# A two-layer SWA, mLSTM and FoX trunk: layer 0's attention stage regrouped with a gate block between its parts and q, k turned by DMA, layer 1's last joins and scores placed earlier

## The chip, the cores and the metric

The kernel runs on one core of a Trainium2 chip. The core has five engines, each with its own instruction stream: TensorE (PE, matmuls; PEld is its weight load), VectorE (DVE), ScalarE (ACT), GpSimd (POOL) and SyncE (SP, which here only issues DMAs). The metric is the device time of one execution in microseconds, as the median of several runs.

## The reference

A trunk of two residual layers over 256 tokens of width 2048, in fp32. Each layer is a mixer and a SwiGLU feed-forward block of hidden width 5632, each behind an RMSNorm. Layer 0's mixer splits one projection into a sliding-window attention (16 query heads of 64, 4 key heads, window 128) and an mLSTM (4 heads, q and k of 128, v of 256); layer 1's mixer is a causal attention with a forget-gate bias (16 heads of 128).

```python
def swa_mlstm_mixer(xn, w_in, w_out, sinks, b_i, b_f, head_gain):
    proj = xn @ w_in
    q_s, k_s, v_s, q_m, k_m, v_m, o_m, i_m, f_m = split_cols(proj, EVEN_SIZES)
    attn = sliding_window_attention(q_s, k_s, v_s, sinks)        # heads reshaped
    i_pre = softcap(i_m + b_i)
    f_pre = softcap(f_m + b_f)
    h = mlstm_chunkwise(q_m, k_m, v_m, i_pre, f_pre)             # chunks of 128
    h = rms_norm(h, head_gain)
    mem = jax.nn.sigmoid(o_m) * h
    return jnp.concatenate([attn, mem], axis=-1) @ w_out
...
def forgetting_attention_mixer(xn, w_in, b_f, w_out):
    q, k, v, f = split_cols(xn @ w_in, FOX_SIZES)
    c = cumsum(log_sigmoid(f + b_f))
    s = q @ k.T * scale + c[:, None] - c[None, :]                # causal mask
    return softmax(s) @ v @ w_out
```

## The kernel before

Every fp32 product is made of three fp32r products. A chunk of weights (256 rows by 512 columns, 512 KB) is loaded by SP into one of four `raw` buffers (L117, `load_raw`); ACT casts it to `hi` (L169), DVE subtracts to `lo` (L170), both in `split_chunk`; PE then does hi by hi, lo by hi and hi by lo (L197 to L199 in `gemm`). A chunk in `gemm` is 12 matmuls of 512 columns: two row blocks, two halves of the tokens, three products. Activations are kept split too, as `xh`, `xl` for the normed input and `mh`, `ml` for the mixer's output; `split_plain` (L295 on ACT, L296 on DVE) makes those. Where two projections of the same input are due (q with k, the two halves of v), `pair_group` does them with seven products instead of eight per two by two blocks; it needs four banks for `plain`, four for `prods`, and at its end `c` is put together from `prods` (L551 to L555) and `fold` adds `plain` (L684, L685). PSUM has two pools of four banks, `pa` (tag acc) and `pm` (tag pm). Names such as `h<-prod` in the profile stand for `c` where a tile lies in the room of another.

Layer 0's order before: K and V of the sliding-window attention, the first eight query heads (`acc1`), then groups 0 and 1 one after the other (`swa(g, qn)`: scores with L319 and L326, softmax with exps L349 on ACT and the products with 1/den L362 on DVE, transposes of the probabilities L371 and L375 copied by ACT L372 and DVE L376, products with v L379 and L380), then the second projection of queries, and groups 2 and 3 with two gate blocks of 256 columns (`tacc`, `oacc`) between their steps. The mLSTM's gates follow: sigmoid (L806), tanh, exp and ln on ACT, the prefix sums through small matmuls `pu`, `pn`, `pb` (L827 to L870), two scans on DVE, the decay matrix `dt_` (L873, L881). Then the q,k group, whose 16 blocks and four of `qsc` are transposed on PE (`ptm`, L307) and copied by DVE (L308), with the 512-column gate block `oacc` in pieces between them; then the scores `pq` (L927), the value group, and the heads with the first chunks of the output projection `begun0`.

Layer 1 has four groups of four heads. q and k of a group are turned by DMA: `turn_heads` copies the two 16-bit halves of each number to planes (ACT, L1094), SP issues a DMA transpose for each plane (L248), and `join` puts them together (two copies for each of q and k, ACT, L1103). The starts and joins of a group are handed out as `steps` during the next group's work; for the last group they are issued in a `while` loop after the last `values` and `begin` parts. `begin(m, k0, k1)` does k0 to k1 of the layer's output projection for column block m; `attend` is a generator whose steps are scores and softmax, transposes, products with v.

The order on each engine comes from the tile scheduler, which orders instructions by data, buffers and a timeline of its own; `tc.issue_after(ins)` puts what is issued inside behind a given instruction. Engines run their streams in order, so an instruction that waits holds all behind it on its engine. `raw` has four buffers, `hi` and `lo` six; the `raw` of pairs (`rb`) come from a room of two.

Of the kernel before, what the change touches and what calls it, by code (L numbers as in the profile page):

```python
# [7 lines left out]
F32 = mybir.dt.float32  # L8
# [9 lines left out]
P = 128  # L18
D = 2048
S = 256  # L20
# [44 lines left out]
def trunk(  # L65
# [94 lines left out]
    last_exp = [None]  # L160

# [4 lines left out]
    def split_chunk(raw, n):  # L166
        hi = wp.tile([P, CK, NB], F32R, tag="hi", name="hi")
        lo = wp.tile([P, CK, NB], F32R, tag="lo", name="lo")
        latest[0] = nc.scalar.copy(hi[:, :, 0:n], raw[:, :, 0:n])  # L169
# [124 lines left out]
    def split_plain(dst_h, dst_l, src):  # L294
        nc.scalar.copy(dst_h, src)  # L295
        nc.vector.tensor_tensor(out=dst_l, in0=src, in1=dst_h.bitcast(F32), op=ALU.subtract)  # L296
# [13 lines left out]
    def attention(sp, q_of, k_of, v_of, dv, scale, bias0, bias1, k_tile, sinks=None, negc=None, s=None, ps=((pm, "pm"), (pm, "pm"))):  # L310
# [48 lines left out]
        for b in range(NT):  # L359
            for j in range(4):  # L360
                e = s[j % 2][:, j // 2, parts[b]]
                nc.vector.tensor_scalar(e, e, rec[:, b, j : j + 1], None, op0=ALU.mult)  # L362
# [132 lines left out]
    def pair_group(room, par, lhs, sums, mats, order, todo=(), row=lambda k: k):  # L495
# [5 lines left out]
        for pos, (kind, pair) in enumerate(order):  # L501
# [21 lines left out]
            hg, lg = split_chunk(ra, NB)  # L523
            run_due(todo, pos)
            t4 = room.t4()
            nc.vector.tensor_tensor(out=t4[:, 0, :], in0=rb[:, 0, :], in1=ra[:, 0, :], op=ALU.subtract)
            nc.vector.tensor_tensor(out=t4[:, 1, :], in0=rb[:, 1, :], in1=rb[:, 0, :], op=ALU.subtract)
            hu = wp.tile([P, CK, NB], F32R, tag="hi", name="hi")
            lu = wp.tile([P, CK, NB], F32R, tag="lo", name="lo")
            split_plain(hu[:, 1, :], lu[:, 1, :], rb[:, 1, :])  # L530
# [176 lines left out]
    with tc.tile_pool(name="ev", bufs=1) as ev:  # L707
# [21 lines left out]

        with tc.tile_pool(name="sw", bufs=1) as sw:  # L730
# [62 lines left out]
            gemm(oacc, x_of, wi, c_o, 256, 0, 4, KT)  # L793
            next(two, None)
            gemm(oacc, x_of, wi, c_o, 256, 4, 8, KT)
            next(three_)
            gemm(oacc, x_of, wi, c_o, 256, 8, 12, KT)
            next(three_, None)
            gemm(oacc, x_of, wi, c_o, 256, 12, KT, KT)

        og = ev.tile([P, NT, ML_H * VD], F32, name="og")

        def gate_out(acc, c0, n):
            for t in range(NT):
                o = og[:, t, c0 : c0 + n]
                nc.scalar.activation(o, acc[t][:, 0:n], AF.Sigmoid, scale=r[:, t : t + 1])  # L806
                nc.gpsimd.tensor_tensor(out=o, in0=o, in1=gain[:, c0 : c0 + n], op=ALU.mult)

        acc = tacc
        gates = ev.tile([P, NT, 8], F32, name="gates")  # L810
        for t in range(NT):
            nc.vector.scalar_tensor_tensor(
                out=gates[:, t, :], in0=acc[t][:, 256:264], scalar=r[:, t : t + 1], in1=bias_g, op0=ALU.mult, op1=ALU.add
            )
        gate_out(acc, 768, 256)
        gate_out(oacc, NB, 256)
        nc.scalar.activation(gates, gates, AF.Tanh, scale=1.0 / CAP)
        nc.vector.tensor_scalar(gates, gates, CAP, None, op0=ALU.mult)
        ig = gates[:, :, 0:4]
        nlf = ev.tile([P, NT, 4], F32, name="nlf")  # L820
        nc.scalar.activation(nlf, gates[:, :, 4:8], AF.Exp, scale=-1.0)
        nc.scalar.activation(nlf, nlf, AF.Ln, bias=1.0)

        pu = pm.tile([P, NB], F32, tag="pm", name="pu")
        for c in range(NT):
# [468 lines left out]
```

## Time and profile before

Three runs: 2096.64, 2095.11 and 2090.21 us, median 2095.11.

| | us |
|---|---|
| profiled execution | 2096.03 |
| its span | 2094.3 |
| PE busy | 2080.2 |
| DVE busy | 1810.2 |
| ACT busy | 1365.8 |
| weights and other reads from HBM | 408.67 MB, 196 GB/s over the span |

The page gives busy times of engines, the chain that ended last and groups of instructions. Matmuls are pipelined: a matmul of 512 columns has a record of 0.39 us, while the next one starts 0.23 us later, so lengths of PE's work are taken from start to start. The granted clock of TensorE is 1.00 or 0.50; at 0.50 matmuls take twice as long. fp32 matmuls that are not fp32r stand twice in the trace (two passes), once in the program. Rows of the chain of waits name what an engine waited for, in order of time; "DMA raw" there is the time from a load's issue to its landing.

### The profile page before, as it was taken

The numbers are of one execution on the slowest core, as the hardware profiler recorded it, in microseconds if no ns is written. First come the engines' busy times: TensorE is split into PE (matmuls) and PEld (weight loads), VectorE is DVE, ScalarE is ACT, GpSimd is POOL, SyncE is SP. The second block draws the span as 40 slices with busy tenths as digits, with TensorE's granted clock in tenths as the row PEclk, the third lists the DMA queues.
The fourth block names the chain that finished last, engine by engine and source line by source line (L and its number), as shares of the span: only waits on it lengthen the run. The fifth ranks groups of instructions, "written<-read, shape, count | busy, mean of one in ns | idle before, by whom it ended". The sixth has DMA issues, their size and how long they took to land.

```text
span 2094.3 us, 26757 instructions
## 1 busy us (share of the span) xinstructions
PE 2080.2 (99%) x9502; PEld 1727.9 (83%) x9502; DVE 1810.2 (86%) x2400; ACT 1365.8 (65%) x1721; POOL 41.1 (2%) x70
## 2 busy tenths in 40 slices
PE   9999999999999999999999999999999999999998
PEld 7878888888888888888888888788888888888886
DVE  6688758999999998998898777579999999998995
ACT  6565568766567655766867676586766567556763
POOL 2100000000000000000000000000000000000000
PEclk9999999999999999999999999999999999999999
DMA  9446667766676757676787665577766677658763
GB/s 331 120 135 190 215 183 229 249 194 214 205 227 214 215 195 223 212 221 172 205 259 209 201 212 164 170 232 228 241 204 215 197 220 212 228 179 227 220 200 132
DMA packets 304438, 434.56 MB, mean 207 GB/s; under 512 B 102049, under 2 KB 110257, under 8 KB 304305
## 3 DMA queue, kind: packets, MB, share of 16 engines
q1 hardware_dynamic: 302544, 427.05, 65.7%
q0 software_dynamic: 1616, 5.78, 0.8%
q8 instruction: 74, 1.21, 0.2%
q14 instruction: 60, 0.48, 0.1%
q10 hardware_dynamic: 144, 0.03, 0.0%
HBM read 408.67 MB, written 2.11 MB: 196 GB/s over the span
## 4 chain that ended last, share of the span: by engine, by line
PE 94%; DMA 2%; DVE 2%; ACT 1%; issue 1%; SPq 0%; POOLq 0%; POOL 0%; ACTq 0%
PE acc L421 20%; PE acc L420 20%; PE acc L422 20%; PE prod L420 5%; PE prod L421 5%; PE prod L422 5%; PE acc L197 4%; PE acc L199 4%; PE acc L198 4%; PE vacc L199 1%; PE vacc L197 1%; PE vacc L198 1%; DMA raw<-in_w_out_odd_dram 1%; DVE lo L170 1%; PE p L326 0%
## 5 line engine op out<-in xcount | busy, mean ns | idle before, releaser
L169 ACT CAST hi<-raw 128x1024 fp32r<-128x1024 f32 (+1 forms) x664 | 674.4, 1031 | 430.0 <-PE acc L422 247.9
L170 DVE TENSOR_TENSOR lo<-raw,hi 128x1024 fp32r<-128x1024 f32 (+1 forms) x664 | 783.8, 1195 | 149.2 <-ACT hi L169 146.5
L421 PE MATMUL acc<-lo,xh 128*128 128x512 f32 x1204 | 468.7, 389 | 0.5 <-DVE lo L170 0.5
L422 PE MATMUL acc<-hi,xl 128*128 128x512 f32 x1204 | 464.7, 389 | 0.0
L420 PE MATMUL acc<-hi,xh 128*128 128x512 f32 x1204 | 462.1, 389 | 0.0
L421 PEld LDWEIGHTS acc<-lo,xh 128*128 128x128 f32 x1204 | 226.1, 188 | 47.9 <-DVE lo L170 0.8
L422 PEld LDWEIGHTS acc<-hi,xl 128*128 128x128 f32 x1204 | 226.1, 188 | 47.2 <-issue 0.3
L420 PEld LDWEIGHTS acc<-hi,xh 128*128 128x128 f32 x1204 | 226.1, 188 | 46.9
L421 PE MATMUL acc<-lo,mh 128*128 128x512 f32 x444 | 172.7, 389 | 0.0
L422 PE MATMUL acc<-hi,ml 128*128 128x512 f32 x444 | 171.4, 389 | 0.0
L420 PE MATMUL acc<-hi,mh 128*128 128x512 f32 x444 | 169.3, 389 | 0.0
L295 ACT CAST ht<-raw 128x1024 fp32r<-128x1024 f32 x94 | 98.8, 1051 | 58.9 <-DVE raw L532 22.4
L197 PE MATMUL acc<-hi,mh 128*128 128x512 f32 x320 | 126.6, 398 | 3.1 <-ACT mh L295 3.1
L198 PE MATMUL acc<-lo,mh 128*128 128x512 f32 x320 | 125.7, 393 | 0.0
L199 PE MATMUL acc<-hi,ml 128*128 128x512 f32 x320 | 125.0, 393 | 0.0
L295 ACT CAST ht<-t 128x1024 fp32r<-128x1024 f32 x94 | 98.8, 1052 | 39.6 <-PE prod L422 29.3
L296 DVE TENSOR_TENSOR lt<-raw,ht 128x1024 fp32r<-128x1024 f32 x94 | 114.4, 1217 | 5.5 <-ACT ht L295 5.3
L296 DVE TENSOR_TENSOR lt<-t,ht 128x1024 fp32r<-128x1024 f32 x94 | 114.3, 1216 | 1.2 <-ACT ht L295 0.9
L295 ACT CAST hi<-raw 128x512 fp32r<-128x512 f32 x112 | 69.3, 619 | 63.9 <-PE acc L422 48.6
L421 PEld LDWEIGHTS acc<-lo,mh 128*128 128x128 f32 x444 | 83.4, 188 | 17.3
L420 PEld LDWEIGHTS acc<-hi,mh 128*128 128x128 f32 x444 | 83.3, 188 | 17.3
L422 PEld LDWEIGHTS acc<-hi,ml 128*128 128x128 f32 x444 | 83.3, 188 | 17.3
(375 smaller groups left out, 3571.0 us busy)
## 6 DMA issues: line engine op xcount, KB each, us to landing
raw<-in_w_gate_dram SPq DMA_DIRECT2D x176, 512.0 KB, 4.7
raw<-in_w_up_dram SPq DMA_DIRECT2D x176, 512.0 KB, 4.8
raw<-in_w_down_dram SPq DMA_DIRECT2D x176, 512.0 KB, 5.1
raw<-in_w_in_odd_dram SPq DMA_DIRECT2D x88, 512.0 KB, 4.8
raw<-in_w_in_even_dram SPq DMA_DIRECT2D x64, 512.0 KB, 4.6
raw<-in_w_out_even_dram SPq DMA_DIRECT2D x32, 512.0 KB, 4.3
raw<-in_w_out_odd_dram SPq DMA_DIRECT2D x32, 512.0 KB, 5.2
raw<-in_w_in_odd_dram SPq DMA_DIRECT2D x8, 272.0 KB, 3.5
```

What stands on the lines that cost most here:

```text
L169: latest[0] = nc.scalar.copy(hi[:, :, 0:n], raw[:, :, 0:n])
L170: nc.vector.tensor_tensor(out=lo[:, :, 0:n], in0=raw[:, :, 0:n], in1=hi[:, :, 0:n].bitcast(F32), op=ALU.subtract)
L197: nc.tensor.matmul(o, ah[:, ts], hi, start=(k == 0), stop=False)
L198: nc.tensor.matmul(o, ah[:, ts], lo, start=False, stop=False)
L199: last_mm[0] = nc.tensor.matmul(o, al[:, ts], hi, start=False, stop=(k == k_all - 1))
L295: nc.scalar.copy(dst_h, src)
L296: nc.vector.tensor_tensor(out=dst_l, in0=src, in1=dst_h.bitcast(F32), op=ALU.subtract)
L420: nc.tensor.matmul(o, ah, hi, start=start, stop=False)
L421: nc.tensor.matmul(o, ah, lo, start=False, stop=False)
L422: nc.tensor.matmul(o, al, hi, start=False, stop=stop)
```

## The change

It has four parts. (1) Layer 0's sliding-window groups run in pairs: 0 and 1 begin together and the second query projection stands between their steps; 2 and 3 likewise with the gate blocks. (2) The gates' functions move ahead, and the 512-column gate block (`oacc`, OFF_OM) moves from behind the q,k group to between groups 2 and 3, the prefix matmuls and the exps. (3) q and k of the mLSTM are turned by DMA as in layer 1: ACT copies planes to `qmt` and `kmt`, four DMA transposes land in the rooms of `ce` and `ve`, four ACT copies join; starts and joins are handed to the value group (`TURN_QK` = its first four pair steps), and the scores `pq` and the transposes of `qsc` come after that group. The q,k group takes the other bank pools (par 1 for 0). (4) In layer 1, the last group's joins are issued one at a time at parts 5 and 6 of the last loop, the next split of a chunk is held behind each, the last group's scores come before `begin(0, 8, 10)`, and `begin(1, ...)` is cut at 2 and 6 instead of 6 and 10. `late` and `last_mul` are new and not used.

```diff
     def split_chunk(raw, n):
...
-        latest[0] = nc.scalar.copy(hi[:, :, 0:n], raw[:, :, 0:n])
+        with ExitStack() as order:
+            if behind[0]:
+                order.enter_context(tc.issue_after(behind[0].ins))
+                behind[0] = None
+            latest[0] = nc.scalar.copy(hi[:, :, 0:n], raw[:, :, 0:n])
...
-            for g in range(2):
-                for _ in swa(g, qn):
-                    pass
-            qn = natural(sw, project(wi, OFF_QS + NB, NB), NB, "qn")
+            zero, one = swa(0, qn), swa(1, qn)
+            next(zero)
+            next(one)
+            qacc = project(wi, OFF_QS + NB, NB)
+            for gen in (zero, one):
+                next(gen)
+                next(gen, None)
+            qn = natural(sw, qacc, NB, "qn")
...
-            gemm(tacc, x_of, wi, c_t, 264, 0, 2, KT)
             next(two)
-            gemm(tacc, x_of, wi, c_t, 264, 2, 6, KT)
             next(three_)
-            gemm(tacc, x_of, wi, c_t, 264, 6, KT, KT)
+            gemm(tacc, x_of, wi, c_t, 264, 0, KT, KT)
+            gemm(oacc, x_of, wi, c_o, 256, 0, 4, KT)
             next(two)
...
+            gate_out(oacc, NB, 256)
+            oacc = new_acc()
+            gemm(oacc, x_of, wi, OFF_OM, NB, 0, 4, KT)
             next(three_)
-            gemm(oacc, x_of, wi, c_o, 256, 8, 12, KT)
+            gemm(oacc, x_of, wi, OFF_OM, NB, 4, 6, KT)
             next(three_, None)
...
+            gemm(oacc, x_of, wi, OFF_OM, NB, 6, 10, KT)
...
         nc.scalar.activation(ex, ex, AF.Exp)
-
+        gemm(oacc, x_of, wi, OFF_OM, NB, 10, 14, KT)
...
+            gemm(oacc, x_of, wi, OFF_OM, NB, 14, KT, KT)
+            gate_out(oacc, 0, NB)
...
-            plain, c = pair_group(room, 0, x_of, sums_m, [(wi, OFF_QM), (wi, OFF_KM)], QK_ORDER)
+            plain, c = pair_group(room, 1, x_of, sums_m, [(wi, OFF_QM), (wi, OFF_KM)], QK_ORDER)
             fold(plain, c, (rq, r))
-            oacc = [bank(1, "oacc") for _ in range(NT)]
-            gemm(oacc, x_of, wi, OFF_OM, NB, 0, 6, KT)
...
+                for b in range(2):
+                    nc.scalar.copy(flat[:, b, :].rearrange("p (t n) -> p t n", t=NT), cu[:, 2 * m : 2 * m + 2, :, b])
+
+                def start(flat=flat, turned=turned):
+                    with tc.issue_after(load[0].ins):
+                        turn_planes([turned[:, b, :, :] for b in range(2)], flat)
+
+                def join(whole=whole, turned=turned):
+                    cb = whole.rearrange("p (n b) -> p n b", b=2)
+                    for b in range(2):
+                        nc.scalar.copy(
+                            cb[:, :, b].rearrange("p (g t q) -> p g t q", g=4, t=NT),
+                            turned[:, b, :, :].rearrange("p (t g) q -> p g t q", t=NT),
+                        )
...
-            for dst, src in ((qmt, qm), (kmt, km)):
-                for g in range(0, ML_H, 2):
-                    transpose_many(
-                        dst[:, g : g + 2, :].rearrange("p g (t q) -> p (g t) q", q=P),
-                        [src[:, t, (g + i) * QK : (g + i + 1) * QK] for i in range(2) for t in range(NT)],
-                        (pa, "acc"),
-                    )
...
-            plain, c = pair_group(room, 0, x_of, sums_m, [(wi, OFF_VM), (wi, OFF_VM + NB)], QK_ORDER)
+            plain, c = pair_group(
+                room, 0, x_of, sums_m, [(wi, OFF_VM), (wi, OFF_VM + NB)], QK_ORDER, list(zip(TURN_QK, starts + joins))
+            )
...
+                if i == 3 and n in (5, 6):
+                    with tc.issue_after(last_exp[0].ins):
+                        run_next(steps)
+                    behind[0] = last_join[0]
                 part()
...
-        while steps:
-            with tc.issue_after(last_exp[0].ins):
-                run_next(steps)
+        split2 = last_split[0]
         begun[1] = new_acc()
...
-        begin(0, 8, 10)
         with tc.issue_after(last_mm[0].ins):
             next(gen)
+        begin(0, 8, 10)
+        behind[0] = split2
         begin(0, 10, 12)
-        begin(1, 0, 6)
+        begin(1, 0, 2)
         next(gen)
-        begin(1, 6, 10)
+        begin(1, 2, 6)
         next(gen, None)
-        begin(1, 10, 12)
+        begin(1, 6, 12)
```

How the scheduler's order moves is shown at three places. The first is ACT in layer 1, from the exps of the third group on (a row is an operation, `hi<-raw` a cast of a weight chunk, `heads` a join, `t<-pp` the copy of the transposed probabilities, `mh<-po` the split of the attention's output). Before, L-numbers of the kernel before:

```order
L349 ACTIVATE s,den<-s,neg 128x256 x4
L169 CAST hi<-raw 128x1024 x4
L1103 COPY heads<-t_11220 128x1024 x2
L1103 COPY heads<-turned 128x1024 x2
L372 COPY t_11453<-pp 128x512 x2
L169 CAST hi<-raw 128x1024 x5
L295 CAST mh<-po 128x512 x2
L1036 ACTIVATE vn<-vacc,r 128x256 x2
```

And now (L1130 is the join, L176 the cast):

```order
L356 ACTIVATE s,den<-s,neg 128x256 x4
L176 CAST hi<-raw 128x1024
L1130 COPY heads<-t_11208 128x1024 x2
L176 CAST hi<-raw 128x1024
L1130 COPY heads<-turned 128x1024 x2
L176 CAST hi<-raw 128x1024 x2
L379 COPY t_11441<-pp 128x512 x2
L176 CAST hi<-raw 128x1024
L302 CAST mh<-po 128x512 x2
```

The four joins stood together behind four casts; now one cast stands ahead of the first two, one between the pairs, and five casts in place of nine stand ahead of `mh`.

The second place is PE in layer 0, at the prefix matmuls (`pu`, `pn`, `pb` are the gates' small products, `acc<-hi,xh` and its like a chunk of the 512-column gate block, `po` the products with v). Before:

```order
L380 MATMUL po<-t_1232,vs 64x128
L845 MATMUL pn<-ident,mt 128x4
L846 MATMUL pn<-ident,edge 128x4
L844 MATMUL pn<-nlf,upper 128x4
L845 MATMUL pn<-ident,mt 128x4
L846 MATMUL pn<-ident,edge 128x4
L870 MATMUL pb<-mt,sel 128x256 x4
L420 MATMUL acc<-hi,s_1388 128x512
L421 MATMUL acc<-lo,s_1388 128x512
```

And now:

```order
L204 MATMUL acc<-hi,xh 128x512
L205 MATMUL acc<-lo,xh 128x512
L859 MATMUL pn<-ident,mt 128x4
L860 MATMUL pn<-ident,edge 128x4
L858 MATMUL pn<-nlf,upper 128x4
L859 MATMUL pn<-ident,mt 128x4
L860 MATMUL pn<-ident,edge 128x4
L887 MATMUL pb<-mt,sel 128x256 x4
L206 MATMUL acc<-hi,xl 128x512
L204 MATMUL acc<-hi,xh 128x512
```

`pu`, which before directly preceded these with eight rows of `po`, now lies 28 matmuls of the gate block ahead of the first `pn` with `mt`; the q,k group that followed `pb` at once now follows ten more matmuls.

The third place is the value group, on SP (loads of weight chunks and the DMA transposes) and on ACT (`qmt<-h` the plane copies of q, `qmt<-ce` the joins). SP now, where before stood 38 loads from `in_w_in_even` in a row and no transposes:

```order
L117 DMA raw<-in_w_in_even_dram 128x2x512 x32
L255 DMA_TRANSPOSE ce<-qmt 128x8x128 x2
L255 DMA_TRANSPOSE ve<-kmt 128x8x128 x2
L117 DMA raw<-in_w_in_even_dram 128x2x512 x6
L117 DMA raw<-in_w_out_even_dram 128x2x512 x23
```

ACT now:

```order
L927 COPY qmt<-h 128x1024 x2
L927 COPY kmt<-h 128x1024 x2
L176 CAST hi<-raw 128x1024
L302 CAST mh<-raw 128x1024
L176 CAST hi<-raw 128x1024
L936 COPY qmt<-ce 128x1024 x2
L302 CAST hi<-raw 128x512
L936 COPY kmt<-ve 128x1024 x2
L302 CAST mh<-h 128x1024
L176 CAST hi<-raw 128x1024 x2
```

The last six loads of the group stand behind the four transposes on SP, and the casts of the group's later chunks stand behind the joins on ACT. PE loses its 16 `ptm<-ident,h` transposes.

More of the change, by code (lines that the diff above doesn't have):

```diff
@@ L798, in trunk @@
             next(three_, None)
[L799 to L810, printed above, removed]
@@ L821, in trunk @@
[L821 to L825, printed above, removed]
-            uo = pu[0:4, c * P : (c + 1) * P]
-            nc.tensor.matmul(uo, ig[:, c, :], ident, start=True, stop=False)
-            nc.tensor.matmul(uo, nlf[:, c, :], upper, start=False, stop=True)
-        nc.tensor.matmul(pu[0:4, 2 * P : 2 * P + 1], nlf[:, 0, :], ones[:, 0:1], start=True, stop=True)
@@ L839, in trunk @@
[L839 to L841 removed]
+            pu = pm.tile([P, NB], F32, tag="pm", name="pu")
+            for c in range(NT):
+                uo = pu[0:4, c * P : (c + 1) * P]
+                nc.tensor.matmul(uo, ig[:, c, :], ident, start=True, stop=False)
+                nc.tensor.matmul(uo, nlf[:, c, :], upper, start=False, stop=True)
+            nc.tensor.matmul(pu[0:4, 2 * P : 2 * P + 1], nlf[:, 0, :], ones[:, 0:1], start=True, stop=True)
```

138 lines of the change are left out of this document (78 added, 60 removed).

## The prediction

> **What bounds the kernel now.** I read the page's head and busy times first, then the chain of waits, then a windows view cut at the changes of the granted clock.
>
> ```profile
> span 2094.3 us, 26757 instructions
> PE 2080.2 (99%) x9502; PEld 1727.9 (83%) x9502; DVE 1810.2 (86%) x2400; ACT 1365.8 (65%) x1721; POOL 41.1 (2%) x70
> PE 94%; DMA 2%; DVE 2%; ACT 1%; issue 1%; SPq 0%; POOLq 0%; POOL 0%; ACTq 0%
> ```
>
> PE is busy for 99% of the span and holds 94% of the chain, so an edit can gain in two ways only: fewer matmuls, or less of PE's time lost to waits and half clock. How much is lost, and where, the windows show (columns: stretch, length, then busy us and instructions of PE, PEld, DVE, ACT, POOL, then the granted clock, DMA share, GB/s).
>
> ```profile
> 80.00:143.37 63.37, 62.71 (x428) 52.55 (x428) 52.50 (x108) 43.47 (x98) 5.59 (x8) 1.00 0.48 146
> 143.37:146.78 3.41, 3.41 (x26) 2.90 (x23) 2.49 (x11) 1.10 (x2) 0.11 (x1) 1.00 0.00 0
> 146.78:150.19 3.41, 3.41 (x9) 2.26 (x8) 2.91 (x10) 2.54 (x9) 0.00 (x0) 0.50 0.00 0
> 150.19:153.60 3.41, 3.41 (x10) 2.64 (x9) 2.71 (x6) 2.94 (x5) 0.00 (x0) 0.50 0.00 0
> 153.60:300.00 146.40, 146.40 (x671) 121.23 (x670) 112.42 (x157) 80.44 (x111) 9.24 (x10) 1.00 0.63 194
> 300.00:1140.00 840.00, 840.00 (x3755) 697.65 (x3754) 768.39 (x978) 570.59 (x661) 4.21 (x6) 1.00 0.70 215
> 1310.73:1314.14 3.41, 1.22 (x6) 0.79 (x5) 1.67 (x3) 2.56 (x5) 0.00 (x0) 1.00 0.82 293
> 1314.14:1317.55 3.41, 3.41 (x9) 2.72 (x9) 2.16 (x3) 1.17 (x2) 0.00 (x0) 0.50 0.90 324
> ```
>
> Most of the kernel runs as the row from 300 us does: 3755 matmuls in 840 us, 0.224 us each, with nothing to win. The two layers' attention stages are the exception. In layer 0 PE idles 63.37 - 62.71 = 0.66 us before 143.4, and from 146.78 it runs 6.82 us at clock 0.50, which costs half of that, 3.41. So at most 4.1 us can come back there. Ahead of the half clock stands a stretch of 26 tiny matmuls (143.37), in layer 1 one with PE busy for 1.22 of 3.41 us. Either can take the clock down.
>
> In layer 1 the chain of waits (start, length, what) and PE's timeline tell why:
>
> ```profile
> 1299.40 1.14 ACT heads L1103
> 1300.62 2.96 ACT heads L1103 x3
> 1304.25 1.05 ACT t L372 x2
> 1305.30 0.96 ACT hi L169
> 1306.28 1.24 DVE lo L170
> 1307.53 3.94 DMA raw<-in_w_out_odd_dram
> 1311.58 1.04 ACT hi L169
> 1312.62 0.49 ACT mh L295
> 1318.46 0.23 PE acc L199
> 1335.22 7.44 DMA raw<-in_w_out_odd_dram
> 1342.77 1.04 ACT hi L169
> ```
> ```profile
> 1310.58 0.39 PE L199 MATMUL acc<-hi,ml 128*128 128x512 f32 x1
> 1313.16 0.50 PE L197 MATMUL acc<-hi,mh 128*128 128x512 f32 x1 [2.19 <-ACT mh L295]
> 1344.35 0.50 PE L197 MATMUL acc<-hi,mh 128*128 128x512 f32 x1 [0.88 <-ACT mh L295]
> ```
>
> ACT first does four joins in a row (1.14 + 2.96 us), so the casts of the weight chunks start 5 us late, the raw slots come free late, the load that goes into one of them lands late (1307.53 + 3.94), and the cast that waits for it stands ahead of `mh` on ACT, for which PE waits. A matmul of 512 columns takes 0.23 us from start to start, so PE could have gone on at 1310.81 and went on at 1313.16: 2.35 us lost. The window at half clock behind it loses 1.71, and the second place of the same kind 0.88. Layer 1's stock is therefore 4.9 us.
>
> **The change part by part.** *Transposes removed.* 16 transposes of q and k leave PE.
>
> ```profile
> 186.13 1.69 PE L307 MATMUL ptm<-ident,h 128*128 128x128 f32 x14
> ```
>
> 14 of them, the last 0.27 long by the tile's own row, take (1.69 - 0.27)/13 = 0.11 us each: -1.8 us. This is sure, since PE is the bound. DVE loses four copies, off the path.
>
> *Layer 1's joins.* Each join now stands between casts: cast, two joins, cast, two joins, casts. The joins' 4.1 us are the same, and the third chunk's `lo` comes 0.6 us after PE asks for it by my walk through the new order with these rows' lengths; then casts and loads run ahead. Between the last group's scores and its transposes there are now 87 matmuls (19.7 us) instead of 55. Behind these transposes only 3 matmuls (0.7 us) stand before the products with v, which need ACT's two copies (1.05 us, row 1304.25) and a DVE copy of 0.7; the copies start while the last seven transposes (0.8 us) still run, so that wait is at most 0.3. I take -4.9 + 0.6 = -4.3. Bounds: -4.9 if nothing waits, and -1 if the late load only moves (the long landing of 7.44 us against 3.94 is 3.5 us, more than the lead that a cast gains).
>
> *Layer 0's attention and the filler.* The 512-column gate block (96 matmuls) moves from behind the q,k group to between the small matmuls of groups 2 and 3 and the gates. In the new order the `pn` rows have chunks of it on both sides, so a stretch like 143.37 disappears and with it the half clock: up to -4.1. What comes in exchange is DVE. Between the `s`-by-`rec` products of group 3 and the second `dt_` addition, DVE now has the gate prefix, two `t4` subtractions that wait for weight loads, and five splits.
>
> ```profile
> 138.33 1.93 DVE L362 TENSOR_SCALAR s<-s,rec 128x128 f32<-128x128 f32 x8
> L170 DVE TENSOR_TENSOR lo<-raw,hi 128x1024 fp32r<-128x1024 f32 x27 | 32.5, 1217 | 4.6 <-ACT hi L169 4.4
> L526 DVE TENSOR_TENSOR h<-raw 128x512 f32<-128x512 f32 x5 | 3.4, 683 | 0.1
> raw<-in_w_in_even_dram SPq DMA_DIRECT2D x64, 512.0 KB, 4.6
> ```
>
> With 5 operations of 1.2, ten of 0.7 and some twenty short ones DVE needs some 16 us, and the two loads issued behind a split land 4.6 us after it. PE has 23 us of matmuls in this stretch, of which the first 5 pass before the first load lands. The two meet almost exactly: I find 0.2 us at `po` of group 2 (ACT's copy behind a second table load), 0.4 at the bank of the first `dt_` addition and 0.2 at the end of the value group, 0.8 together, and take 1.3 since the two loads are read at their median. Bounds: 0, and 4.1 if they land like the 7.44 us row (2.8 later each, once on the path). Part: -4.1 + 1.3 = -2.8.
>
> Layer 0 gets four more table loads on ACT, because sigmoid, exp and ln now alternate.
>
> ```profile
> L806 ACT ACT_TABLE_LOAD x3 | 3.8, 1283 | 0.1
> ```
>
> At 1.283 us each they add 5.1 us to an engine with 43.47 of 63.37 us busy in the first row of the windows; one of the four lies on group 3's exps and is in the 0.2 at `po`. The Trainium skill speaks against this edit: "ScalarE: Activation LUTs", section "Table sets: the hidden batching unit", asks to do all functions of one set before the next and puts a load at about 2.7 us. By that figure the wait at `po` would grow by some 1.4 us and the sum come to 2088.5; the row's 1.283 contradicts the figure, and the sum goes by the row.
>
> *q and k by DMA.* SP issues four transposes inside the value group, between the loads of its weights, and ACT does four plane copies before and four joins after them.
>
> ```profile
> 1281.37 2.60 SPq L248 DMA_TRANSPOSE t<-heads  x2
> 1284.01 2.66 SPq L248 DMA_TRANSPOSE turned<-heads  x2
> t<-heads SPq DMA_TRANSPOSE x2, 2.8
> turned<-heads SPq DMA_TRANSPOSE x2, 4.5
> L1094 ACT COPY heads<-c 128x1024 uint16<-128x1024 uint16 x4 | 4.0, 1042 | 0.0
> L1103 ACT COPY heads<-t 128x1024 uint16<-128x1024 uint16 x2 | 2.6, 1346 | 0.0
> ```
>
> On SP they take 5.3 us, and the loads of the third pair of chunks queue behind them. On ACT they take 4.2 + 5.3 us. From the end of `fold` I add up: copies 4.2, transposes issued as the copies end, last landing 4.5 later, joins; the cast of the chunk behind them ends some 2.7 us before PE asks for it. So this costs nothing while that cover of 2.7 us lasts. Without it each us late is a us of PE, and past some 2.2 us idle in one window the half clock follows (1.7 a window).
>
> **The sum**, against the profiled execution's own 2096.03 us (span 2094.3, and 1.7 around it): -1.8 - 4.3 - 2.8 = -8.9, so 2087.1. That execution lies 0.9 above the median of the runs shown (2095.11), so the change is -8 against the median. I predict 2087.
>
> The clock decides 3.4 + 1.7 of these. The windows at 0.50 have a length of 3.41 us. The Trainium skill, "TensorE: Matmul & The Clock Gate", section "Part 1: The HAM clock gate (the "warmup" mystery)", gives a free-running window of 3413 ns, which agrees, and says that an idle window throttles; the row at 143.37 disagrees, because PE counts as busy in all of it. By the page alone no half clock could come back in layer 0 after this change; by the rows it can, which is the second rival.
>
> **The rivals.** *Layer 1's load only moves* (10%). For it: PE's second wait hangs on a load of 7.44 us, and joins between casts delay single casts. Against: three casts now precede PE's need. Layer 1 then gives 1 instead of 4.3: 2090.4.
>
> *Layer 0 keeps its losses* (20%). For it: the 16 us of DVE work behind two loads, which has no slack. Against: the same kind of subtraction waits 0.1 us in all now (row L526). It decides when the loads land 2.8 us later than the median: 4.1 us of waits, and with an idle of 2.2 us in a window also two windows at half clock, 3.4. Layer 0's part is then -4.1 + 4.1 + 3.4 = +3.4 instead of -2.8: 2093.3.
>
> *Transposes hold SP and ACT* (12%, slower). Should the four transposes run one after the other and not overlapped, at the 4.5 us of the row 18 us pass from the first copy's end to the last landing, instead of 3.1 + 4.5 = 7.6. ACT stands in front of the second join for 10.4 us more, with the casts of the next chunks behind it; after the cover of 2.7 PE idles 7.7 and has two windows at half clock, 3.4. The loads behind the transposes suffer the same on SP: their engines are taken, and where they are also late by one more landing (4.6) the value group waits again. 7.7 + 3.4 + 4.6 = 15.7: 2087.1 + 15.7 = 2102.8. The kernel is as slow as before at 9 us of such waits and measurably slower at 14. For it: SP issues in order, and both joins stand ahead of casts. Against: in the rows two issued 1.3 us apart land at medians of 2.8 and 4.5, so they overlap.
>
> **How the numbers follow.** Forecast 58%, the rivals 10, 20 and 12%. About 0.3%, 6.3 us, is what a measurement of this kernel tells from no change, so faster means below 2088.8 and slower above 2101.4. Faster: nine tenths of the forecast, a quarter of the first rival and little of the second, 0.56. Slower: most of the third rival and a tail of the second, 0.12. The rest, 0.32, is within. Range: the floor is everything won, 2096.03 - 1.8 - 4.9 - 4.1 = 2085.2, less 2 for the spread of the runs: 2083. Upwards it takes in the first two rivals and their spread and leaves out the third: 2097. Of the forecast's own cases most lie in 2084 to 2090.
>
> **What would show it.** Right: no clock of 0.50 between 60 and 300 us nor between 1290 and 1350; no PE wait on `mh` above 0.7 us in layer 1; PE 16 matmuls shorter, the transposes of `ce` and `ve` landing in 3 to 5 us, the cast after the second join ended before PE needs it. The wait that I expect instead is PE on DVE (`dt_` or `lo`) near 155 us. The forecast is wrong if windows at 0.50 stand around 145 to 160 or 205 to 220 us, if PE waits for `hi` behind the joins of q and k, or if a load from `in_w_out_odd_dram` still ends a wait of more than 1 us.

## The result, and the profile after

The changed kernel takes 2087.44 us (median of 10 runs, 2085.75 to 2089.08), the kernel before, run beside it, 2092.09 us (10 runs, 2090.19 to 2096.64): a ratio of 0.9974, 95% interval 0.9965 to 0.9984. It is faster by 4.7 us, 0.26%. The profiled execution of after took 2087.40 us with a span of 2085.6. The profiled execution of before, on which the prediction's sum stands, had a span of 2094.3, so the two traces differ by 8.7. That execution of before lay 3.9 us above the median of its kernel, so the rest of this text compares trace with trace and median with median.

The page of after, its head, its busy times and its chain of waits by engine:

```profile
span 2085.6 us, 26737 instructions
PE 2074.6 (99%) x9486; PEld 1723.5 (83%) x9486; DVE 1803.8 (86%) x2396; ACT 1378.9 (66%) x1733; POOL 51.6 (2%) x70
PE 98%; DMA 1%; DVE 0%; ACT 0%; issue 0%; POOLq 0%; POOL 0%; SPq 0%; DVEq 0%; ACTq 0%
```

PE now holds 98% of the chain instead of 94%. Of its waits between 60 us and the end of layer 1's attention one is left (the row has what PE waited for, then us in total, how often, the longest):

```profile
PE acc L427 <- DVE u L562: 0.2, 1, 0.2
```

The windows of after, cut at its own clock changes (columns as in the prediction):

```profile
80.00:142.69 62.69, 62.69 (x437) 53.63 (x436) 47.55 (x99) 47.73 (x102) 7.53 (x8) 1.00 0.52 153
142.69:146.10 3.41, 3.41 (x19) 2.65 (x17) 3.41 (x12) 0.98 (x2) 0.00 (x0) 1.00 0.42 144
146.10:149.52 3.42, 3.42 (x18) 2.74 (x18) 3.39 (x7) 2.55 (x3) 0.76 (x1) 1.00 0.48 151
149.52:152.94 3.42, 3.42 (x10) 2.64 (x9) 3.42 (x11) 1.56 (x2) 0.77 (x1) 0.50 0.01 2
152.94:300.00 147.06, 147.06 (x664) 121.52 (x664) 110.16 (x157) 96.49 (x136) 7.20 (x10) 1.00 0.64 198
1304.00:1345.00 41.00, 41.00 (x199) 34.56 (x198) 27.37 (x41) 23.21 (x42) 0.00 (x0) 1.00 0.59 193
```

In both stages PE is busy without a gap. Layer 1 has lost its half clock. Layer 0 has kept one window of it (149.52) where before had two in a row. PE's timeline ahead of that window:

```profile
145.34 0.38 PE L859 MATMUL pn<-ident,mt 4*128 4x4 f32 x2
...
146.66 1.97 PE L887 MATMUL pb<-mt,sel 4*128 4x256 f32 x8
148.56 0.50 PE L206 MATMUL acc<-hi,xl 128*128 128x512 f32 x1
...
149.67 0.63 PE L427 MATMUL acc<-hi,xh 128*128 128x512 f32 x1
```

The filler does stand on both sides of the small products, and the clock falls all the same: a 512-column matmul takes 0.50, then 0.63 us.

Where the 8.7 us went is seen from how far the same DVE instructions lie earlier than in the trace of before (the median of each stretch, us; a start-up difference of up to 0.8 can be in every row, as the row "layer 1 only" shows, whose layer 0 is that of before). The first stretch lies behind layer 0's attention, the second ahead of layer 1's last groups, the third behind them; "layer 1" is the third less the second:

```
               320-400  1180-1260  1360-1420  layer 1  half-clock windows in layers 0, 1
after            -4.7      -3.8       -8.9      -5.2      1, 0   (before: 2, 1)
after, again     -5.2      -4.5       -9.1      -4.6      1, 0
layer 0 only     -5.0      -4.5       -4.6      -0.1      1, 1
layer 1 only     -0.8      -0.4       -5.1      -4.7      2, 0
joins only       -3.5      -3.1       -6.0      -2.9      2, 0
scores only      -5.1      -4.7       -9.8      -5.1      0, 0
turns on PE      -3.4      -3.0       -7.6      -4.6      1, 0
pb on 128 rows   -5.4      -4.7       -9.5      -4.8      0, 0
same in before   -3.6      -3.4       -4.5      -1.1      0, 1
```

Against this one trace of before, layer 0 gives 4 to 5 us and layer 1 about 5. The 0.3 to 0.9 us that every kernel gives back between the first two stretches was not followed up.

### The profile page after: what moved, and what is told of

Read it like the earlier page. It is cut to its first block, busy times and chain, and to the rows that moved or that the text cites. A ratio compares the mean times of both kernels' runs of the same rounds, so it can differ in the third digit from the quotient of the medians.

```text
span 2085.6 us, 26737 instructions
## 1 busy us (share of the span) xinstructions
PE 2074.6 (99%) x9486; PEld 1723.5 (83%) x9486; DVE 1803.8 (86%) x2396; ACT 1378.9 (66%) x1733; POOL 51.6 (2%) x70
## 4 chain that ended last, share of the span: by engine, by line
PE 98%; DMA 1%; DVE 0%; ACT 0%; issue 0%; POOLq 0%; POOL 0%; SPq 0%; DVEq 0%; ACTq 0%
PE acc L427 20%; PE acc L428 20%; PE acc L429 20%; PE acc L205 5%; PE acc L206 5%; PE acc L204 5%; PE prod L427 5%; PE prod L428 5%; PE prod L429 5%; PE vacc L206 1%; PE vacc L204 1%; PE vacc L205 1%; PE p L333 1%; PE po L386 1%; PE pp L378 0%
## 5 line engine op out<-in xcount | busy, mean ns | idle before, releaser
L176 ACT CAST hi<-raw 128x1024 fp32r<-128x1024 f32 (+1 forms) x664 | 674.0, 1030 | 406.0 <-PE acc L429 239.7
```

## The experiments

All kernels compute the whole of the reference.

**Layer 0's half alone.** The changed kernel with the end of layer 1 written as before:

```diff
-                if i == 3 and n in (5, 6):
-                    with tc.issue_after(last_exp[0].ins):
-                        run_next(steps)
-                    behind[0] = last_join[0]
...
+        while steps:
+            with tc.issue_after(last_exp[0].ins):
+                run_next(steps)
...
+        begin(0, 8, 10)
         with tc.issue_after(last_mm[0].ins):
             next(gen)
-        begin(0, 8, 10)
-        behind[0] = split2
         begin(0, 10, 12)
-        begin(1, 0, 2)
+        begin(1, 0, 6)
```

> The changed kernel with layer 1's last group as it was before. Theory (the two layers' gains are independent, layer 0 gave 4.2 us and layer 1 4.8 by the shift of like instructions between the two traces): the span is 2094.3 - 4.2 = 2090.1, PE waits for mh again twice (about 2.2 and 0.9 us) and one window at clock 0.50 stands again near 1310. Rival (layer 1's gain came from the state in which layer 0 leaves the loads): the span stays near 2086.

2090.98 us (2090.38 to 2094.15; ratio 0.9997, 0.9987 to 1.0006), span 2089.5. ACT of this kernel, then PE at the matmul that waits:

```profile
1301.44 3.90 ACT L176 CAST hi<-raw 128x1024 fp32r<-128x1024 f32 x4
1307.61 1.04 ACT L176 CAST hi<-raw 128x1024 fp32r<-128x1024 f32 x1 [2.27 <-DMA raw<-in_w_out_odd_dram]
1308.57 1.07 ACT L302 CAST mh<-po 128x512 fp32r<-128x512 f32 x2
```
```profile
1309.20 0.59 PE L204 MATMUL acc<-hi,mh 128*128 128x512 f32 x1 [2.78 <-ACT mh L302]
```

The loss of before is back: five casts ahead of `mh`, the fifth waiting for its load, PE idle for 2.78 us and one window at half clock. The second wait of before (0.88) did not return. By the medians this half is worth only 1.9 us (before, run beside it, 2092.90), and the interval takes in no change at all: the 4.8 us by the spans hold against the one trace of before.

**Layer 1's half alone.** The kernel before with the same lines of layer 1 taken over.

> The kernel before with the change in layer 1 alone. Theory: the span is 2094.3 - 4.8 = 2089.5, the two windows at clock 0.50 near 147 to 154 us stay, none stands in layer 1. Rival (the gains depend on each other): 2091 or more.

2089.85 us (2087.86 to 2093.13; ratio 0.9990, 0.9980 to 0.9999), span 2089.2: PE waits for `mh` nowhere, and layer 0 has its 6.83 us at half clock as before. The two halves add up: 4.8 + 5.1 = 9.9 us of span alone against 8.7 together, a difference of less than one half-clock window. By the medians they are 1.9 and 3.1, 5.0 together, against 4.7.

**The joins' place alone.** The changed kernel, its joins between the casts as in the change, but the last group's scores and the chunks around them cut as before:

```diff
+        begin(0, 8, 10)
         with tc.issue_after(last_mm[0].ins):
             next(gen)
-        begin(0, 8, 10)
-        behind[0] = split2
         begin(0, 10, 12)
-        begin(1, 0, 2)
+        begin(1, 0, 6)
         next(gen)
-        begin(1, 2, 6)
+        begin(1, 6, 10)
```

> The changed kernel, of layer 1's edits only the joins between the casts; the last group's scores and the cuts of begin(1, ...) as before. Theory (the four joins in a row make the load late): the first wait on mh and the half clock behind it stay away, the second wait (0.9) may come back: span 2085.6 to 2086.5. Rival (the scores' earlier place and the longer filler behind them give the gain): span 2089 or more.

2088.41 us (2086.83 to 2090.47; ratio 0.9985, 0.9975 to 0.9994), span 2088.2. ACT, then PE:

```profile
1300.36 2.01 ACT L176 CAST hi<-raw 128x1024 fp32r<-128x1024 f32 x2
1303.91 1.04 ACT L176 CAST hi<-raw 128x1024 fp32r<-128x1024 f32 x1 [1.54 <-DVE lo L177]
1305.92 1.05 ACT L176 CAST hi<-raw 128x1024 fp32r<-128x1024 f32 x1 [0.97 <-DMA raw<-in_w_out_odd_dram]
1307.91 1.04 ACT L176 CAST hi<-raw 128x1024 fp32r<-128x1024 f32 x1 [0.93 <-PE acc L206]
1308.86 1.07 ACT L302 CAST mh<-po 128x512 fp32r<-128x512 f32 x2
```
```profile
1309.49 0.50 PE L204 MATMUL acc<-hi,mh 128*128 128x512 f32 x1 [1.61 <-ACT mh L302]
```

The theory of the prediction falls here. The casts do run ahead, as it said, but there are still five of them in front of `mh`, the last three each held by something else, and PE waits 1.61 us. The joins alone are worth 2.9 by the shifts above, of the 4.9 that the prediction had in stock, and 1.7 of these came because the half clock stayed away.

**The scores' place alone.** The changed kernel with the new place and cuts of the scores, but the four joins in a row as before:

```diff
-                if i == 3 and n in (5, 6):
-                    with tc.issue_after(last_exp[0].ins):
-                        run_next(steps)
-                    behind[0] = last_join[0]
...
+        while steps:
+            with tc.issue_after(last_exp[0].ins):
+                run_next(steps)
```

> The changed kernel, of layer 1's edits only the scores' earlier place and the new cuts; the four joins in a row as before. Theory: the wait of 2.2 us on mh and one window at 0.50 (1.7 us) come back, the second wait does not: span 2085.6 + 4.0 = 2089.6. Rival (the scores' place gives the gain): 2085.6 to 2086.5.

2086.41 us (2085.01 to 2087.64; ratio 0.9974, 0.9965 to 0.9984), span 2084.6. ACT:

```profile
1301.21 1.05 ACT L176 CAST hi<-raw 128x1024 fp32r<-128x1024 f32 x1
1302.69 0.59 ACT L302 CAST mh<-po 128x512 fp32r<-128x512 f32 x1 [0.42 <-PE po L387]
1304.00 0.59 ACT L302 CAST mh<-po 128x512 fp32r<-128x512 f32 x1 [0.72 <-PE po L387]
...
1305.20 3.90 ACT L176 CAST hi<-raw 128x1024 fp32r<-128x1024 f32 x4
1311.19 1.05 ACT L176 CAST hi<-raw 128x1024 fp32r<-128x1024 f32 x1 [2.09 <-DMA raw<-in_w_out_odd_dram]
```

The rival holds. The joins are where they were, a cast still waits 2.09 us for its load, and it costs PE nothing, because `mh` now stands ahead of it, behind one cast in place of five. PE never waits for `mh`. The scores' place, the new cuts of `begin` and the split that is held back went in together; they were not tried one by one.

**q and k turned on PE.** The changed kernel with the transposes of before, 16 on PE, in place of the planes, DMA transposes and joins:

```diff
+            for dst, src in ((qmt, qm), (kmt, km)):
+                for g in range(0, ML_H, 2):
+                    transpose_many(
...
-                room, 0, x_of, sums_m, [(wi, OFF_VM), (wi, OFF_VM + NB)], QK_ORDER, list(zip(TURN_QK, starts + joins))
+                room, 0, x_of, sums_m, [(wi, OFF_VM), (wi, OFF_VM + NB)], QK_ORDER
```

> The changed kernel with q and k of the mLSTM transposed on PE again, right after fold and ahead of the value group's first pair step; no planes, DMA transposes or joins. Theory (the DMA way costs PE nothing and saves 16 transposes of 0.11 us): 1.8 us more and whatever PE waits for fold and DVE's copies, span 2087.4 to 2088.5. Rival (the four transposes on SP and the eight copies on ACT cost something): span 2086.5 or less.

2088.6 us (2086.58 to 2090.4; ratio 0.9978, 0.9969 to 0.9988), span 2086.7. That is 1.2 above after by the medians and 1.1 by the spans, with one half-clock window in both. The intervals overlap, so only the sign and the rough size are borne out. By the shifts of the first stretch the way over PE costs 1.3 more than after and 1.8 more than its second trace, each with one half-clock window there, so 1.1 to 1.8 is what can be said.

**Each DMA transpose twice.** The changed kernel, with every transpose of q and k planes issued a second time into the same place:

```diff
-                        turn_planes([turned[:, b, :, :] for b in range(2)], flat)
+                        for _ in range(2):
+                            turn_planes([turned[:, b, :, :] for b in range(2)], flat)
```

> The changed kernel with each of the four DMA transposes of q and k issued twice, which holds SP for 5.4 us more ahead of six loads and moves the second join by about 5 us. Theory (the cover in the changed trace is 3.1 us, from the end of the cast of the first chunk behind the joins to the matmul that uses it): PE waits some 2.3 us, span 2087.9, up to 2089.6 with a window at half clock. Rival A (later loads have more room than that, the cover is over 5.4): 2085.6. Rival B (transposes run one after the other and hold the loads): PE waits 5.4 or more, 2091 or more.

2097.5 us (2095.86 to 2099.31; ratio 1.0022, 1.0012 to 1.0032), span 2095.3: 9.7 above after, where 2.3 were expected. SP, ACT and PE of this kernel, and its windows:

```profile
200.23 5.90 SPq L255 DMA_TRANSPOSE ce<-qmt  x4
206.23 6.54 SPq L255 DMA_TRANSPOSE ve<-kmt  x4
212.83 8.34 SPq L117 DMA_DIRECT2D raw<-in_w_in_even_dram  x6
```
```profile
229.82 1.05 ACT L176 CAST hi<-raw 128x1024 fp32r<-128x1024 f32 x1 [2.00 <-DMA raw<-in_w_out_even_dram]
230.78 0.58 ACT L561 COPY h<-prod 128x512 f32<-128x512 f32 x1
```
```profile
PE acc L204 <- DVE ve L1000: 3.3, 1, 3.3
PE pq L1024 <- DVE dt__1518 L1025: 1.9, 1, 1.9
PE prod L427 <- ACT mh L302: 1.2, 1, 1.2
PE acc L427 <- ACT hi L176: 0.2, 1, 0.2
```
```profile
236.63:240.04 3.41, 1.48 (x10) 1.02 (x10) 2.75 (x5) 1.90 (x3) 0.00 (x0) 1.00 0.85 255
240.04:250.28 10.24, 6.95 (x21) 5.41 (x20) 7.48 (x12) 2.62 (x4) 3.00 (x4) 0.50 0.67 216
```

The waits that the theory priced are the last two, 1.4 us, right behind the joins. The rest came some 20 us later: the loads behind the transposes are issued late on SP (from 212.83, in after from 206.37), the casts that wait for them stand on ACT ahead of the copy `h<-prod` that ends the value group (in after it starts at 227.71, here at 230.78), and PE then waits 1.9 and 3.3 us and is busy for 6.95 us at half clock, which costs 3.5. 1.4 + 5.2 + 3.5 = 10.1; the spans differ by 9.7. That the late loads are due to SP's queue is read from the order on SP; that the transposes' own transfers also slow the loads was not tried apart.

**The pairs of `pb` apart.** The changed kernel with four 512-column matmuls between the two pairs of `pb`:

```diff
-                for i in range(2):
+                with tc.issue_after(last_mm[0].ins):
+                    for i in range(2):
...
+                if g == 0:
+                    gemm(oacc, x_of, wi, OFF_OM, NB, 14, KT, KT)
```

> The changed kernel with the two pairs of pb matmuls (contraction over 4 rows) apart: four 512-column matmuls between them, the second pair behind the gate block's end. Theory (the one window at clock 0.50 left in layer 0 comes from a 3.41 us window in which pn and pb, matmuls that use little of the array, make up 2.5 us): with about 2 us of them in any window the half clock stays away and the span is 2085.6 - 1.7 = 2083.9. Rival (2 us are still enough, or something else takes the clock down): one window at 0.50 stays, span 2085.6.

2087.41 us (2085.96 to 2090.22; ratio 0.9978, 0.9969 to 0.9988), span 2085.4; the window at half clock stays, from 150.01. Four large matmuls between the small ones are not enough.

**`pb` over 128 rows.** The changed kernel, where `pb` contracts over 128 rows of which 124 are zeros, in place of 4. The products and their number are the same:

```diff
-            mt = ev.tile([4, S], F32, name="mt")
+            mtp = ev.tile([P, S], F32, name="mt")
+            nc.gpsimd.memset(mtp, 0.0)
+            mt = mtp[0:4, :]
...
-        sel = ev.tile([4, ML_H, P], F32, name="sel")
+        sel = ev.tile([P, ML_H, P], F32, name="sel")
...
-                        pb[:, i, :, :].rearrange("p c q -> p (c q)"), sel[:, 2 * g + i, :], mt, start=True, stop=True
+                        pb[:, i, :, :].rearrange("p c q -> p (c q)"), sel[:, 2 * g + i, :], mtp, start=True, stop=True
```

> The changed kernel with the pb matmuls contracted over 128 rows, 124 of them zero, instead of 4: same number of matmuls, same columns, same result. In all traces so far a window of 3.41 us is followed by one at clock 0.50 where columns times rows of its matmuls come to 0.32 or less of a full array, and is not where they come to 0.36 or more. Theory (the clock goes by the array's rows and columns that matmuls use): the window with pn and pb rises above 0.5, no window at 0.50 in layer 0, span 2083.9, and the median 1.7 below the changed kernel's of the same call. Rival (zeros do no work, or the count is by instructions): one or two windows at 0.50 stay, same time as the changed kernel.

2086.11 us (2085.3 to 2087.38; ratio 0.9970, 0.9957 to 0.9982), span 2084.7; no half clock between 60 and 1345 us. PE's timeline:

```profile
146.77 1.99 PE L889 MATMUL pb<-mt,sel 128*128 128x256 f32 x8
...
149.53 0.39 PE L427 MATMUL acc<-hi,xh 128*128 128x512 f32 x1
```

`pb` takes as long as with four rows (1.99 against 1.97 us), and the matmul behind it runs at full clock. One trace without half clock proves little, since that of the scores' place alone, with four rows, has none in layer 0 either. The granted clock on record for every execution says more. In the thirteen traces it goes with the number of half-clock windows ahead of the kernel's end: 0.999 with none, 0.998 with one, 0.997 with two, 0.996 with three, 0.995 with four. Here it is 0.999 in all six executions, and 0.999 in one of the 19 executions of the unpadded change. The shares 0.32 and 0.36 of the expectation do not come out of the rows; the section on the clock below has the ones that do.

**Both: the scores' place and `pb` over 128 rows.** The edits of those two kernels together.

> The same as e8_pb_rows, with layer 1's four joins in a row again and only the scores' place and the cuts changed. Theory (the joins' place gives nothing once mh no longer stands behind the casts): the same time as e8_pb_rows within 0.5 us. Rival (the joins' place gives part of the gain, hidden in one run by the half clock of layer 0): 1 us or more above e8_pb_rows.

2086.35 us (2085.08 to 2087.97; ratio 0.9969, 0.9957 to 0.9980), span 2084.4. With or without the joins between the casts the time is the same within 0.3 us: beside the scores' place the joins' place gives nothing that can be measured.

**`pb` over 128 rows in the kernel before.** The same three lines there, nothing else.

> The kernel before with nothing but pb over 128 rows. Theory: the two windows at 0.50 near 147 to 154 us go, 3.4 us, span 2090.9; layer 1 as before. Rival (before's stretch of small matmuls is long enough without pb): one or two windows stay, 2092.6 to 2094.3.

2089.57 us (2088.95 to 2092.62; ratio 0.9988, 0.9979 to 0.9997), span 2090.0. Its windows over layer 0's attention, and over the one half clock that is left, layer 1's:

```profile
60.00:300.00 240.00, 239.36 (x1254) 199.08 (x1253) 184.68 (x317) 142.21 (x253) 16.62 (x23) 1.00 0.55 167
...
1310.94:1314.35 3.41, 3.41 (x9) 2.63 (x8) 1.91 (x3) 1.04 (x1) 0.00 (x0) 0.50 0.83 307
```

The half clock of layer 0 is gone without any filler. The median is 3.4 us below that of before in the same comparison (2092.98); the ratio of 0.9988 makes it 2.5 us, with an interval from 0.6 to 4.4. The granted clock was 0.999 in 7 of these 11 executions and in 2 of the 21 of before.

**The changed kernel again**, beside the last three.

> The changed kernel once more, beside the others on the same chip: span 2084 to 2087, with none, one or two windows at 0.50 in layer 0, as the window's phase falls; 2087.4 as the median.

2088.1 us (2086.14 to 2088.45; ratio 0.9971, 0.9962 to 0.9981), span 2086.4, one half-clock window from 147.82. The version with `pb` over 128 rows is 2.0 us below it by the medians, of which 1.7 is that window, but the ratios to before, 0.9970 and 0.9971, do not tell them apart. It and the two versions with the scores' place have the lowest medians of all that were run, 0.26 to 0.31% below the kernel before by the ratios.

## Why the prediction was right, and where its reasons were not

**The sum.** -8.9 was predicted against the profiled execution and -8.7 found in the spans; 2087 was predicted and 2087.44 measured. That the time is so near is partly luck. The prediction started from a median of 2095.11 for the kernel before, out of three executions, and forecast -8 against it. Ten executions gave 2092.09, 3.0 lower, and the change of the medians is -4.7, 3.4 less than forecast: two errors that cancel. By the granted clocks most of both has one source, the half clock. The sum takes the three half-clock windows of the profiled execution, 5.1 us, as lost in every execution. By their granted clocks (0.999 for no window to 0.996 for three, as in the traces), the 76 executions of before that ran beside the experiments had no window 11 times, one 20 times, two 35 times and three 10 times, 1.6 on average, and the 19 of the changed kernel 1.1. This is an estimate, as the clock is on record to three places. It leaves some 0.8 us of gain from the clock, where the two traces, with three windows and one, show 3.4.

**Layer 1 (-4.3): size right, cause wrong.** The shift is 5.2, and the loss that the prediction described (2.35 + 1.71 + 0.88) is gone. Not all of that loss is there in every execution: the second wait, 0.88, is missing in the kernel before with `pb` over 128 rows, whose layer 1 was not changed, and in the kernel with layer 0's half alone. The step that failed is the paragraph on layer 1's joins, which lets the casts and loads "run ahead" once the joins stand between casts. With this alone PE still waited 1.61 us for `mh`; with the scores' earlier place alone it did not wait, joins or no joins. What decides is how many casts stand between the transposed probabilities and `mh` on ACT. It is five in the four traces where PE waits for `mh` there (before, the same with `pb` over 128 rows, layer 0's half alone, the joins' place alone; 1.6 to 2.8 us), and one in the other nine, where PE does not wait. After has one:

```profile
1299.68 1.07 ACT L176 CAST hi<-raw 128x1024 fp32r<-128x1024 f32 x1
1303.65 0.58 ACT L302 CAST mh<-po 128x512 fp32r<-128x512 f32 x1 [2.90 <-PE po L387]
1304.96 0.59 ACT L302 CAST mh<-po 128x512 fp32r<-128x512 f32 x1 [0.72 <-PE po L387]
...
1306.17 3.89 ACT L176 CAST hi<-raw 128x1024 fp32r<-128x1024 f32 x4
1312.11 1.06 ACT L176 CAST hi<-raw 128x1024 fp32r<-128x1024 f32 x1 [2.05 <-DVE lo L177]
```

In after ACT waits for `po` and not PE for `mh`; a later cast waits 2.05 us, behind `mh` instead of ahead of it. The order rows ahead of the prediction showed both moves side by side; of the second, the walk asked only what wait it might add (at most 0.3), not what it would gain. Its sign "a load from `in_w_out_odd_dram` still ends a wait of more than 1 us" was badly put for the same reason: such a wait is still there on ACT (1.85 us ahead of the cast at 1317.61) and costs nothing. The 0.6 for the third chunk's `lo` did not come.

**Layer 0 (-2.8): sum about right, both terms off.** The wait on DVE, priced at 1.3, did not come: PE waits 0.2 us between 60 and 1345 (in three other traces also 0.7 on DVE's `ve`, some 80 us later than the place that was named). In its place one window at half clock stayed, 1.7, so that the sign "no clock of 0.50 between 60 and 300" failed. The stock of 4.1 less 1.7 and 0.2 is 2.2. With 1.1 to 1.8 for the transposes that makes 3.3 to 4.0 against the shift of 4.7; up to 0.8 of the rest may be the start-up, and what is left of it stays open. The failed step is that chunks of the filler on both sides mean that the stretch "disappears and with it the half clock": the small products still stand close together for some 3 us (rows 145.34 to 148.56), and that decides.

**The clock.** All thirteen traces obey one rule. In each window of 3.41 us between 60 and 2070 us, in the phase of the kernel's own clock changes, the time that PE spends on each matmul, times its contraction rows over 128, is added up as a share of the window. A matmul's time runs from its start to the start of the next, or to its own end where PE then idles; idle time counts nothing, and four rows count 1/32. The shares are worked out from the records behind PE's timeline:

```
kernel             window from   share   clock of the next window
pb apart              146.6      0.49    0.50
layer 1 only          142.6      0.46    0.50
transposes twice      236.6      0.43    0.50
before                143.4      0.39    0.50
before               1310.7      0.36    0.50
after                 146.1      0.33    0.50
layer 0 only         1306.0      0.19    0.50
joins only           1308.0      0.56    1.00
scores only           147.0      0.58    1.00
scores only           143.6      0.60    1.00
transposes twice      216.2      0.60    1.00
pb on 128 rows        144.4      0.70    1.00
before               1341.4      0.74    1.00
```

All 13 windows at full clock with a share of at most 0.49 are followed by half clock, and none with 0.55 or more is. An idle PE (1310.7, 1306.0) and a PE that is busy with thin matmuls (143.4, 146.1) come to the same. A window at half clock was followed by another when its share was 0.62 or less (5 windows) and by full clock at 0.90 or more (13 windows). The windows' phase is not tied to the program: the same layer 0 with the filler showed none, one or two windows at half clock (seven traces: 0, 1, 1, 1, 1, 1, 2), the one without because a window's edge cut the small products in two (0.60 and 0.58). This moves single executions by 1.7 us a window. With `pb` over 128 rows in the changed kernel the share between 60 and 1345 us is at least 0.65 wherever the window lies; with four rows, in after's trace, it would be 0.18 for a window from 145.2. That contraction rows count is shown by changing them alone; whether the columns of the array that a matmul uses count as well was not tried. The Trainium skill, "TensorE: Matmul & The Clock Gate", section "Part 1: The HAM clock gate (the "warmup" mystery)", has the length of the window right (3413 ns; the rows show 3.41 us); its idle window is one case of what is seen here, where PE's record is busy throughout the windows from 143.4 and 146.1.

**Transposes and their cover (-1.8 and 0).** The gain on PE is 1.1 to 1.8, no nearer to be told. The cover was priced at 2.7 us. SP, the landings (median us), ACT and PE of after:

```profile
200.78 2.71 SPq L255 DMA_TRANSPOSE ce<-qmt  x2
203.54 2.72 SPq L255 DMA_TRANSPOSE ve<-kmt  x2
206.37 9.15 SPq L117 DMA_DIRECT2D raw<-in_w_in_even_dram  x6
```
```profile
ce<-qmt SPq DMA_TRANSPOSE x2, 3.4
ve<-kmt SPq DMA_TRANSPOSE x2, 3.3
```
```profile
209.26 2.56 ACT L936 COPY kmt<-ve 128x1024 uint16<-128x1024 uint16 x2
...
212.63 1.99 ACT L176 CAST hi<-raw 128x1024 fp32r<-128x1024 f32 x2
```
```profile
216.74 0.40 PE L427 MATMUL acc<-hi,xh 128*128 128x512 f32 x1
```

The first cast of the last row of ACT ends near 213.6 and PE asks at 216.74: a cover of 3.1. The slower rival's mechanism is real all the same. Doubling the transposes set it off, and it cost four times what was expected, because the delay did not end with the join but went on through SP's loads to the end of the value group.

**The other rivals.** "Layer 1's load only moves" is out: no wait of PE for `mh` is left anywhere in after. "Layer 0 keeps its losses" came true for one of the two windows at half clock, through the small products and not through DVE. The table loads cost PE nothing that shows. The four of L745 take 1283 ns each, and behind nine of layer 0's ten loads ACT's next instruction starts within 0.02 us, so of the 2.7 us for a load that the Trainium skill, "ScalarE: Activation LUTs", section "Table sets: the hidden batching unit", gives, the traces show 1.28.

## What to carry to other kernels

On an engine that works in order, count what stands in front of the instruction that the bottleneck waits for, before asking whether the things in front are late: a cast that waits for a load cost nothing behind that instruction and 1.6 to 4.5 us ahead of it (idle and half clock). When PE is busy and the clock still halves, weigh its matmuls by their contraction rows: padding a thin contraction with zeros cost PE no time and gave 2.5 to 3.4 us in the kernel before, while moving 96 matmuls left a window at half clock. Where windows at half clock come and go between executions, one profiled execution is no base for a sum: read the granted clock of the others first. A step that is hidden has a cover that can be read off (3.1 us here), but the price of exceeding it must be followed past the next buffer, since the late loads and not the late join cost most.

## What the runs showed of the hardware

A matmul over 4 rows counts for the clock as next to nothing although PE is busy with it: with the same 256 columns and the same time (1.97 and 1.99 us for eight), 4 rows were followed by half clock in nine of ten traces and 128 rows, mostly zeros, in none of three, in two kernels. Half clock followed every full-clock window of 3.41 us in which the time on matmuls, weighted by rows, was at most 0.49 of the window, and none with 0.55 or more. Two SBUF-to-SBUF DMA transposes of 128 x 1024 elements of 16 bit occupy SP's queue for 2.71 us and land after 3.3 to 3.4 us, four of them for 5.90 to 6.54 us, and the loads behind them on the queue are issued only then (206.37 and 212.83).
